# First MLP of a two-layer diffusion block: hidden features completed and squared in their PSUM bank, with all their low parts on VectorE

## The chip, the cores and the metric

The kernel runs on one core of one Trainium2 chip. The metric is the device time of one execution in microseconds (us), as the median over runs. The engines are TensorE (PE; its weight loads are shown apart as PEld), VectorE (DVE), ScalarE (ACT), GpSimd (POOL) and SyncE (SP), which issues most of the DMAs. Each engine works through its own queue in order; semaphores order the engines among each other.

## The reference

Two layers (DEPTH = 2) work on 512 latent tokens x and 256 context tokens ctx of 1024 features, in float32. The change touches the MLP at the end of a layer alone. The context tokens go through the MLP of layer 0 only, since nothing reads them after layer 1.

```python
def squared_relu_mlp(h, w1, w2):
    return jnp.square(jax.nn.relu(h @ w1)) @ w2
...
    for l in range(DEPTH):
...
            h_ctx = h_ctx + cg2 * rmsnorm(squared_relu_mlp(hc2, w_ff1[l], w_ff2[l]), g_post_ff[l])
...
        hx2 = rmsnorm(x, g_pre_ff[l]) * (1.0 + sc2) + sh2
        x = x + g2 * rmsnorm(squared_relu_mlp(hx2, w_ff1[l], w_ff2[l]), g_post_ff[l])
```

## The kernel before

**Two parts.** TensorE takes float32r operands, which hold fewer bits than float32. So each operand is kept as a high part (a copy that is rounded to float32r) and a low part (the value minus the high part), and a product is three products: high by high, high by low, low by high.

**The MLP.** The 4096 hidden features go in 16 groups of 256. In each layer groups 0 and 1 are plain products (`ff1`, L1099 on; tiles h000c, h011x and so on: layer, group, half of the features, kind of token). They are made of 24 matmuls each, for the 256 context tokens (layer 0 only) and for two halves of the latent tokens. Groups 2 to 15 (`wino`, L1171 on) use Winograd's form of Strassen's product for the latent tokens: seven products of twelve matmuls (called 11, 21, t1, t2, t3, t4, 22; tiles w and wt) over sums of weights and sums S of token blocks, from which additions make four quadrants c11, c22, c21 and c12. In layer 0 two plain products for the context tokens (`plain`, tiles wc) come with each group. `hidden` (L1118 on) takes a quadrant or a plain product, and makes Relu (ScalarE), the square as high part (ScalarE, into the tile hx or hc), the square again in place (ScalarE), and the difference as low part. `ff2` then multiplies the hidden features of a group with its rows of w_ff2 (tiles f200x for group 0 and so on) and VectorE adds the result to Y.

**Memory.** PSUM has two banks with the tag S, two with T, three with F and one with V. The plain products of groups 0 and 1 use S alone; the products of `wino` alternate between S and T, so a product takes the bank of the one four before it, where no other step takes a T. The second products use F. Temporaries in SBUF come from the tags h1, h2 and h3 with two buffers each, and the tiles of a tag are handed out in the order of the program text. r of `hidden` is an h1, p1 and u4 are h2, the quadrants c11, c22 and c21 are h3. The sums S of the token blocks (`wino_a`, L943 on, called once before group 2) go through s1 (h1), s2 (h2) and s3 (h3). In layer 0 two of the four etiles and one of the two ptiles hold sums for the rest of the layer. So hx and hc of a group take the buffers of the group before, and are written when its second products have read them.

**Order.** A scheduler sets the order of each engine's queue from the program text, the dependences, the priorities (`tc.high_priority(offset=HP)` around `wino`) and its own estimates of the durations. Second products of one group and first products of the next are therefore mixed. GpSimd and VectorE share the low parts by the table LOADS; its entry for the hidden features of layer 0 is "vpvpvv": two of six on GpSimd. Beside the MLP of layer 0 run the modulations of layer 1: VectorE sums rows of w_ada (L264, L266), as each load arrives.

Of the kernel before, what the change touches and what calls it, by code (L numbers as in the profile page):

```python
# [11 lines left out]
F32 = mybir.dt.float32  # L12
# [6 lines left out]
P = 128  # L19
# [12 lines left out]
# How far the first product of the MLP goes ahead of other work.  # L32
HP = 5
# The engine (v or p) that takes each of the two-operand steps of a hidden group: low parts of the weights of the
# first and second product, differences of weights, low parts of the hidden features.
# [10 lines left out]
# What the tensor engine does beside the attention units of a layer: U, G, F load the weights of a column group  # L46
# of the in-projection and u, g, f project a token block with them, fc, fx step through the Fourier mixing,
# gc, gx load the gates, oc, ox step through the output projection, ada through a modulation.
# [13 lines left out]
def _bc(ap, n, axis):  # L62
    """ap with a broadcast dimension of n put in at free position `axis`."""
    v = ap.unsqueeze(axis)
    shape = list(v.shape)
    shape[axis] = n
    return v.to_broadcast(shape)
# [3 lines left out]
def kernel(ctx: ExitStack, tc: tile.TileContext, a: dict, out: bass.AP):  # L71
# [15 lines left out]
    # Temporaries of a chain come from h1, h2, h3 in this order, so that chains never wait in a circle.  # L87
# [9 lines left out]
    # Streams that run side by side have tiles of their own; within a tag tiles are handed out in program order.  # L97
# [35 lines left out]
    # ------------------------------------------------------------- constants  # L133
# [18 lines left out]
    def rows_in(name, width, pairs):  # L152
        """Rows at given partitions of a zeroed [32, width] tile."""
# [6 lines left out]
    def turned(t, name, use):  # L160
        """Feature-major pieces of four chunks of such rows in PSUM, handed to `use`."""
# [7 lines left out]
    # silu(c), silu(c_ctx) as two columns of a zero-padded stationary operand  # L169
# [37 lines left out]
    # ---------------------------------------------------- common small helpers  # L207
# [4 lines left out]
    def power(o, i, scale, bias, expo):  # L212
        """o = (i * scale + bias) ** expo"""
# [11 lines left out]
    def wunit(src, shape, name, lo_eng=None, part=None, hi_pool=False):  # L225
        """A weight unit in two float32r parts whose sum is the float32 weight."""
# [11 lines left out]
    # ------------------------------------------------------------------ adaLN  # L238
    # modc[l]: feature-major columns for (sh1, sc1, sh2, sc2); gates go to DRAM rows.
# [271 lines left out]
    def layer(l, feats):  # L511
# [659 lines left out]
        def wino(g):  # L1171
# [31 lines left out]
            def tile3(nm_):  # L1203
                return h3([P, n], F32, f"{nm_}{nm}")
# [209 lines left out]
```

## Time and profile before

| | |
|---|---|
| median of 3 runs | 1516.37 us (1515.86 to 1518.47) |
| span of the profiled execution | 1516.8 us |
| TensorE busy | 1429.4 us (94%) |
| VectorE, ScalarE, GpSimd busy | 74%, 49%, 42% |
| MLP of layer 0 in the trace | about 345 to 930 us |
| MLP of layer 1 in the trace | about 1158 us to the end |

The profiled execution has a span of 1516.8 us from its first to its last instruction, 0.4 us more than the median of the runs; no other time of it is given. A busy share is the time in which an engine worked on an instruction. Matmuls overlap in the records: a 128x256 matmul is shown with some 0.28 us, while its successor starts 0.12 us later. In the rows of the trace, "[1.63 <-ACT hi_f L234]" says that the engine was idle for 1.63 us just before the row, until line 234 on ScalarE released it.

### The profile page before, as it was taken

The numbers are of one execution on the slowest core, as the hardware profiler recorded it, in microseconds if no ns is written. First come the engines' busy times: TensorE is split into PE (matmuls) and PEld (weight loads), VectorE is DVE, ScalarE is ACT, GpSimd is POOL, SyncE is SP. The second block draws the span as 40 slices with busy tenths as digits, with TensorE's granted clock in tenths as the row PEclk, the third lists the DMA queues.
The fourth block names the chain that finished last, engine by engine and source line by source line (L and its number), as shares of the span: only waits on it lengthen the run. The fifth ranks groups of instructions, "written<-read, shape, count | busy, mean of one in ns | idle before, by whom it ended". The sixth has DMA issues, their size and how long they took to land. (4 is left out here: it accounts for less than half of the span.)

```text
span 1516.8 us, 24509 instructions
## 1 busy us (share of the span) xinstructions
PE 1429.4 (94%) x9133; PEld 1252.7 (83%) x9133; DVE 1115.8 (74%) x2003; ACT 747.7 (49%) x1673; POOL 644.3 (42%) x608
## 2 busy tenths in 40 slices
PE   7999999999899999999989998999998899999997
PEld 4688798788788878888878887998777788989886
DVE  3366887858687877878777758788757987777685
ACT  3346666556534333343333445476656555554452
POOL 3212636646634333334433546234346644344241
PEclk9999999999999999999999999999998999999999
DMA  9634322435132332325554344213134133223322
GB/s 328 228 122 154 112 74 84 137 115 167 42 100 84 124 111 84 126 70 174 167 172 129 125 160 139 72 55 87 39 100 165 56 112 111 93 89 100 110 84 84
DMA packets 94352, 177.58 MB, mean 117 GB/s; under 512 B 5796, under 2 KB 59524, under 8 KB 94232
## 3 DMA queue, kind: packets, MB, share of 16 engines
q1 hardware_dynamic: 91224, 170.93, 35.0%
q0 software_dynamic: 3008, 5.08, 1.2%
q8 instruction: 72, 1.18, 0.3%
q14 instruction: 48, 0.39, 0.1%
HBM read 166.62 MB, written 9.46 MB: 116 GB/s over the span
## 5 line engine op out<-in xcount | busy, mean ns | idle before, releaser
L1152 POOL TENSOR_TENSOR raw_f<-raw_f,raw_f 128x512 f32<-128x512 f32 x70 | 98.2, 1402 | 107.8 <-DVE raw_f L1152 89.5
L1147 ACT CAST Wf<-raw_f 128x512 fp32r<-128x512 f32 x98 | 60.4, 619 | 118.6 <-DMA raw_f<-in_w_ff 108.4
L266 DVE SCALAR_TENSOR_TENSOR acc<-wa,silu,acc 128x1024 f32<-128x1024 f32 x70 | 96.1, 1391 | 21.7 <-DMA wa<-in_w_ada 21.6
L1148 POOL TENSOR_TENSOR Wf<-raw_f,Wf 128x512 fp32r<-128x512 f32 x28 | 40.1, 1433 | 153.3 <-ACT Wf L1147 153.3
L1195 PE MATMUL wc<-f01c,Wf 128*128 128x256 f32 x672 | 98.5, 286 | 3.4 <-DVE p L1201 3.4
L1195 PEld LDWEIGHTS wc<-f01c,Wf 128*128 128x128 f32 x672 | 91.6, 194 | 7.9 <-DVE p L1201 3.8
L1148 DVE TENSOR_TENSOR Wf<-raw_f,Wf 128x512 fp32r<-128x512 f32 x70 | 62.0, 887 | 41.0 <-ACT Wf L1147 40.9
L234 ACT CAST hi_f<-raw_f 128x1024 fp32r<-128x1024 f32 x72 | 73.8, 1043 | 34.8 <-PE f208c L1247 6.6
L235 POOL TENSOR_TENSOR lo_f<-raw_f,hi_f 128x1024 fp32r<-128x1024 f32 x20 | 54.7, 2735 | 77.7 <-ACT hi_f L234 57.6
L1125 DVE TENSOR_TENSOR hx<-r,hx 128x256 fp32r<-128x256 f32 x98 | 61.5, 630 | 31.2 <-ACT r L1124 31.1
L235 DVE TENSOR_TENSOR lo_f<-raw_f,hi_f 128x1024 fp32r<-128x1024 f32 x52 | 76.6, 1478 | 1.3 <-ACT hi_f L234 1.0
L1123 ACT ACTIVATE hx<-r 128x256 fp32r<-128x256 f32 x112 | 45.4, 413 | 44.4 <-PE f203x L1247 8.7
L1182 PE MATMUL w<-f11x,Wf 128*128 128x256 f32 x336 | 65.1, 283 | 0.0
L1182 PE MATMUL w<-S,Wf 128*128 128x256 f32 x336 | 63.0, 283 | 0.0
L1122 ACT ACTIVATE r<-c 128x256 f32<-128x256 f32 x84 | 34.7, 414 | 55.5 <-DVE c L1201 43.4
L1182 PEld LDWEIGHTS w<-f11x,Wf 128*128 128x128 f32 x336 | 54.7, 191 | 1.5
L1182 PEld LDWEIGHTS w<-S,Wf 128*128 128x128 f32 x336 | 53.0, 191 | 1.7 <-issue 0.4
L1182 PE MATMUL w<-f01x,Wf 128*128 128x256 f32 x336 | 50.4, 284 | 1.9 <-ACT Wf L1147 1.0
L1182 PEld LDWEIGHTS w<-f01x,Wf 128*128 128x128 f32 x336 | 46.4, 191 | 5.3 <-ACT Wf L1147 1.4
L1124 ACT ACTIVATE r<-r 128x256 f32<-128x256 f32 x112 | 45.5, 413 | 1.9
L393 ACT ACTIVATE xvx<-xTx,mod 128x256 f32<-128x256 f32 x64 | 31.6, 560 | 18.2 <-PE xTx L379 11.9
L797 ACT ACTIVATE E0x<-E0x,mx_0x 128x512 f32<-128x512 f32 (+1 forms) x32 | 24.9, 778 | 12.9 <-DVE mx_0x L791 12.7
(1243 smaller groups left out, 4886.1 us busy)
## 6 DMA issues: line engine op xcount, KB each, us to landing
raw_f<-in_w_ff SPq DMA_DIRECT2D x128, 512.0 KB
wa<-in_w_ada SPq DMA_DIRECT2D x80, 512.0 KB
wq<-in_w_ada SPq DMA_DIRECT2D x16, 512.0 KB
raw_out0c<-in_w_out SPq DMA_DIRECT2D x8, 512.0 KB
raw_out0x<-in_w_out SPq DMA_DIRECT2D x8, 512.0 KB
res0x<-xr0x SPq DMA_DIRECT2D x8, 512.0 KB
raw_out1x<-in_w_out SPq DMA_DIRECT2D x8, 512.0 KB
xl0x<-in_x SPq DMA_DIRECT2D x4, 512.0 KB
```

The source lines that it names most:

```text
L234: nc.scalar.copy(hi, raw)
L235: (lo_eng or nc.vector).tensor_tensor(out=lo, in0=raw, in1=hi.bitcast(F32), op=ALU.subtract)
L266: nc.vector.scalar_tensor_tensor(out=acc[r], in0=w, scalar=s, in1=acc[r], op0=ALU.mult, op1=ALU.add)
L1122: nc.scalar.activation(r, src, AF.Relu)
L1123: nc.scalar.activation(hv[:, 0], r, AF.Square)
L1124: nc.scalar.activation(r, r, AF.Square)
L1125: next(lo_h).tensor_tensor(out=hv[:, 1], in0=r, in1=hv[:, 0].bitcast(F32), op=ALU.subtract)
L1147: nc.scalar.copy(t[:, 0], src)
L1148: next(lo).tensor_tensor(out=t[:, 1], in0=src, in1=t[:, 0].bitcast(F32), op=ALU.subtract)
L1152: next(diff).tensor_tensor(out=o, in0=x, in1=y, op=ALU.subtract)
L1182: nc.tensor.matmul(ps, W[w][:, wl, k], A[k // 2][:, k % 2, xh], start=(m == 0), stop=(m == 11))
L1195: nc.tensor.matmul(ps, W[f"{k // 4 + 1}{j + 1}"][:, wl, k % 4], f2["c"].ap(k, xh, 0, CTX), start=(m == 0), stop=(m == 3 * KD - 1))
```

## The change

In layer 0 `hidden` has no tile r any more: Relu and the second square work in place on `src`. That is the PSUM bank of the product for the plain products, and for the quadrants too, since the new function `quadrant` adds the other operand into the bank of the quadrant's last product. The low part reads the bank and is always on VectorE. In layer 1 (`last`) the tiles r stay, the low parts go by the table, and the quadrants lie in h3; the fourth, which was added in place in u4, is now an h3 tile as well. In both layers p1 takes p7 ahead of the quadrant c22 instead of behind it. Comments and doc strings are taken out as well, which moves lines from L1201 on.

```diff
         def hidden(g, kd, j, t0, n, src, nm):
...
             hv = H[g][kd][j][:, :, t0:t0 + n]
-            r = h1([P, n], F32, f"r{nm}")
+            r = h1([P, n], F32, f"r{nm}") if last else src
             nc.scalar.activation(r, src, AF.Relu)
             nc.scalar.activation(hv[:, 0], r, AF.Square)
             nc.scalar.activation(r, r, AF.Square)
-            next(lo_h).tensor_tensor(out=hv[:, 1], in0=r, in1=hv[:, 0].bitcast(F32), op=ALU.subtract)
+            (next(lo_h) if last else nc.vector).tensor_tensor(out=hv[:, 1], in0=r, in1=hv[:, 0].bitcast(F32), op=ALU.subtract)
...
-            def tile3(nm_):
-                return h3([P, n], F32, f"{nm_}{nm}")
+            def quadrant(x, ps, j, t0, name):
+
+                c = h3([P, n], F32, f"{name}{nm}") if last else ps
+                add(c, x, ps)
+                hidden(g, "x", j, t0, n, c, f"{nm}{name}")
 
             p1 = h2([P, n], F32, f"p1{nm}")
             nc.scalar.copy(p1, product("11", a11))
-            p2 = product("21", a12)
-            c11 = tile3("c11")
-            add(c11, p1, p2)
-            hidden(g, "x", 0, 0, n, c11, f"{nm}11")
+            quadrant(p1, product("21", a12), 0, 0, "c11")
             plain(0)
             p5 = product("t1", sums(1))
             add(p1, p1, product("t2", sums(2)))
             u4 = h2([P, n], F32, f"u4{nm}")
             add(u4, p1, p5)
             p7 = product("t3", sums(3))
-            c22 = tile3("c22")
-            add(c22, u4, p7)
-            hidden(g, "x", 1, n, n, c22, f"{nm}22")
             add(p1, p1, p7)
-            p4 = product("t4", a22)
-            c21 = tile3("c21")
-            add(c21, p1, p4)
-            hidden(g, "x", 0, n, n, c21, f"{nm}21")
-            p3 = product("22", sums(4))
-            add(u4, u4, p3)
-            hidden(g, "x", 1, 0, n, u4, f"{nm}12")
+            quadrant(u4, p7, 1, n, "c22")
+            quadrant(p1, product("t4", a22), 0, n, "c21")
+            quadrant(u4, product("22", sums(4)), 1, 0, "c12")
             plain(1)
```

The scheduler makes another order of it. Up to the plain products the queues read the same, and those of the mixing stage of layer 1 do too.

**VectorE, plain products of groups 0 and 1.** L1125 is the low part in `hidden`, L956 and L953 are additions and low parts of the sums S, L396 the low parts of the normalised tokens f01x, L266 the modulation. Before, from the first low part of a latent half (hx<-r000x) on:

```order
L1125 TENSOR_TENSOR hx_4155<-r000x_4329,hx_4155 128x256
L266 SCALAR_TENSOR_TENSOR acc_4726<-wa_4800,silu,acc_4726 128x1024
L266 SCALAR_TENSOR_TENSOR acc_4727<-wa_4800,silu,acc_4727 128x1024
L396 TENSOR_TENSOR f01x_3849<-xvx_4106,f01x_3849 128x2x256
L396 TENSOR_TENSOR f01x_3850<-xvx_4116,f01x_3850 128x2x256
L1125 TENSOR_TENSOR hx_4156<-r001x_4359,hx_4156 128x256
L396 TENSOR_TENSOR f01x_3851<-xvx_4126,f01x_3851 128x2x256
L1125 TENSOR_TENSOR hx_4230<-r010x_4389,hx_4230 128x256
L396 TENSOR_TENSOR f01x_3852<-xvx_4136,f01x_3852 128x2x256
L1125 TENSOR_TENSOR hx_4155<-r000x_4517,hx_4155 128x256
L1148 TENSOR_TENSOR Wf_4827<-raw_f_4820,Wf_4827 128x512
L1152 TENSOR_TENSOR raw_f_4820<-raw_f_4820 128x4x128
```

Now, from the L266 ahead of that low part (hx<-h000x) on:

```order
L266 SCALAR_TENSOR_TENSOR acc_4714<-wa_4788,silu,acc_4714 128x1024
L266 SCALAR_TENSOR_TENSOR acc_4715<-wa_4788,silu,acc_4715 128x1024
L396 TENSOR_TENSOR f01x_3849<-xvx_4106,f01x_3849 128x2x256
L396 TENSOR_TENSOR f01x_3850<-xvx_4116,f01x_3850 128x2x256
L1125 TENSOR_TENSOR hx_4155<-h000x_4300,hx_4155 128x256
L396 TENSOR_TENSOR f01x_3851<-xvx_4126,f01x_3851 128x2x256
L956 TENSOR_TENSOR s_4634<-s_4636,f01x_3851 128x512
L396 TENSOR_TENSOR f01x_3852<-xvx_4136,f01x_3852 128x2x256
L956 TENSOR_TENSOR s_4653<-s_4655,f01x_3852 128x512
L1125 TENSOR_TENSOR hx_4156<-h001x_4329,hx_4156 128x256
L956 TENSOR_TENSOR s_4634<-s_4634,f01x_3851 128x512
L1125 TENSOR_TENSOR hx_4228<-h010x_4358,hx_4228 128x256
```

The low part of h000x stood ahead of two L266 and two L396 and now stands behind them. The first additions L956 now stand among the low parts of the first latent half; before, they came behind the second low part of r010x, that of the second half.

**TensorE, plain products of the context tokens.** h001c and h010c are products of groups 0 and 1, xTx transposes of the normalised latent tokens, f200c second products. Before:

```order
L1106 MATMUL h010c_4232<-f01c_3212,lo_f_4226 128x256
L1106 MATMUL h010c_4232<-f01c_3212,hi_f_4225 128x256 x2
L1106 MATMUL h010c_4232<-f01c_3212,lo_f_4226 128x256
L379 MATMUL xTx_4101<-ident,y0x_3619 128x128
L1247 MATMUL f200c_4425<-hi_f_4294,hc_4154 128x512
L1247 MATMUL f200c_4425<-lo_f_4295,hc_4154 128x512
L1247 MATMUL f200c_4433<-hi_f_4294,hc_4154 128x512
L1247 MATMUL f200c_4433<-lo_f_4295,hc_4154 128x512
L1247 MATMUL f200c_4442<-hi_f_4294,hc_4154 128x512
L1247 MATMUL f200c_4442<-lo_f_4295,hc_4154 128x512
L379 MATMUL xTx_4111<-ident,y0x_3619 128x128
L1106 MATMUL h011c_4262<-f01c_3209,hi_f_4219 128x256 x2
```

Now:

```order
L1106 MATMUL h001c_4186<-f01c_3212,hi_f_4150 128x256 x2
L1106 MATMUL h001c_4186<-f01c_3212,lo_f_4151 128x256
L379 MATMUL xTx_4101<-ident,y0x_3619 128x128
L1240 MATMUL f200c_4417<-hi_f_4290,hc_4154 128x512
L1240 MATMUL f200c_4417<-lo_f_4291,hc_4154 128x512
L1240 MATMUL f200c_4425<-hi_f_4290,hc_4154 128x512
L1240 MATMUL f200c_4425<-lo_f_4291,hc_4154 128x512
L1240 MATMUL f200c_4434<-hi_f_4290,hc_4154 128x512
L1240 MATMUL f200c_4434<-lo_f_4291,hc_4154 128x512
L1106 MATMUL h010c_4230<-f01c_3209,hi_f_4217 128x256 x2
```

The product h010c stood ahead of the first transposition shown and of the six second products; now it stands behind them.

**VectorE, Winograd group 6.** wt are the products t1 to t4, hc the hidden features of the context tokens, lo_f a low part of w_ff2. Before, from the addition of t2 to p on:

```order
L1201 TENSOR_TENSOR p_6254<-p_6254,wt_6332 128x256
L235 TENSOR_TENSOR lo_f_6441<-raw_f_6438,hi_f_6440 128x1024
L1201 TENSOR_TENSOR u_6346<-p_6254,wt_6319 128x256
L1201 TENSOR_TENSOR c_6361<-u_6346,wt_6348 128x256
L1201 TENSOR_TENSOR p_6254<-p_6254,wt_6348 128x256
L1201 TENSOR_TENSOR c_6382<-p_6254,wt_6369 128x256
L1125 TENSOR_TENSOR hx_6225<-r_6363,hx_6225 128x256
L1148 TENSOR_TENSOR Wf_6583<-raw_f_6576,Wf_6583 128x512
```

Now, from the lo_f ahead of that addition on:

```order
L235 TENSOR_TENSOR lo_f_6384<-raw_f_6381,hi_f_6383 128x1024
L1201 TENSOR_TENSOR p_6206<-p_6206,wt_6281 128x256
L1125 TENSOR_TENSOR hc_6175<-wc_6239,hc_6175 128x256
L1201 TENSOR_TENSOR u_6295<-p_6206,wt_6268 128x256
L1201 TENSOR_TENSOR p_6206<-p_6206,wt_6297 128x256
L1201 TENSOR_TENSOR wt_6297<-u_6295,wt_6297 128x256
L1201 TENSOR_TENSOR wt_6316<-p_6206,wt_6316 128x256
L1125 TENSOR_TENSOR hx_6177<-wt_6297,hx_6177 128x256
L1148 TENSOR_TENSOR Wf_6526<-raw_f_6519,Wf_6526 128x512
L1125 TENSOR_TENSOR hx_6176<-wt_6316,hx_6176 128x256
```

The low part of hc is now in this queue, ahead of the additions of t1, t3 and t4; the addition of t3 to p stands ahead of the quadrant c22, and the quadrants are written to wt.

## Rows read from the trace of the kernel before

**Rows 1.** The page's first part: busy time of each engine, its share of the span and its count of instructions.
```profile
PE 1429.4 (94%) x9133; PEld 1252.7 (83%) x9133; DVE 1115.8 (74%) x2003; ACT 747.7 (49%) x1673; POOL 644.3 (42%) x608
```

**Rows 2.** Stretches of the span: start and end, length, busy time (and instructions) of PE, PEld, DVE, ACT and POOL, granted TensorE clock as a share of full speed, DMA share, GB/s.
```profile
357.00:405.00 48.00, 47.57 (x331) 44.47 (x330) 30.74 (x34) 27.59 (x61) 23.60 (x23) 0.98 0.17 56
405.00:890.00 485.00, 457.07 (x2853) 404.13 (x2853) 375.20 (x508) 186.49 (x402) 198.81 (x136) 0.99 0.39 123
1195.00:1487.00 292.00, 287.53 (x1784) 258.73 (x1784) 226.92 (x359) 146.03 (x298) 117.69 (x82) 0.99 0.30 94
424.00:430.00 6.00, 4.05 (x19) 3.55 (x19) 6.00 (x9) 1.04 (x2) 0.00 (x0) 0.75 0.28 87
```

**Rows 3.** Waits of TensorE between 405 and 890 us: who waited for whom, us in total, times, longest.
```profile
PE wc L1195 <- DVE p L1201: 3.4, 2, 2.8
...
PE f205x L1247 <- DVE lo_f L235: 2.3, 1, 2.3
...
PE f206x L1247 <- DVE Y0x L1251: 1.9, 1, 1.9
```

**Rows 4.** TensorE in order of time, 405 to 432 us, the rows with a wait ahead: start, length, operation, count, wait.
```profile
407.81 0.73 PE L1247 MATMUL f201c<-hi_f,hc 128*128 128x512 f32 x2 [1.63 <-ACT hi_f L234]
...
413.60 0.79 PE L1247 MATMUL f201c<-lo_f,hc 128*128 128x512 f32 x1 [3.03 <-DVE lo_f L235]
...
418.69 0.98 PE L1182 MATMUL wt<-S,Wf102t 128*128 128x256 f32 x6 [0.57 <-DVE S L953]
...
420.66 0.98 PE L1182 MATMUL wt<-S,Wf102t 128*128 128x256 f32 x6 [0.99 <-DVE S L953]
...
426.29 2.34 PE L1182 MATMUL wt<-f01x,Wf102t 128*128 128x256 f32 x12 [1.95 <-DVE p L1201]
```

**Rows 5.** VectorE in order of time, 379 to 396 us.
```profile
386.24 0.42 DVE L1125 TENSOR_TENSOR hx<-r000x,hx 128x256 fp32r<-128x256 f32 x1 [6.51 <-ACT r000x L1124]
389.41 0.69 DVE L1148 TENSOR_TENSOR Wf<-raw_f,Wf 128x512 fp32r<-128x512 f32 x1 [2.74 <-ACT Wf L1147]
...
394.38 1.12 DVE L1125 TENSOR_TENSOR hx<-r010x,hx 128x256 fp32r<-128x256 f32 x1 [2.57 <-ACT r010x L1124]
395.54 1.68 DVE L956 TENSOR_TENSOR s<-s,f01x 128x512 f32<-128x512 f32 x1
```

**Rows 6.** VectorE in order of time, 354 to 380 us.
```profile
354.65 2.86 DVE L396 TENSOR_TENSOR f01x<-xvx,f01x 128x512 fp32r<-128x512 f32 x1
...
368.10 0.42 DVE L1125 TENSOR_TENSOR hx<-r000x,hx 128x256 fp32r<-128x256 f32 x1
370.81 2.48 DVE L266 SCALAR_TENSOR_TENSOR acc<-wa,silu,acc 128x1024 f32<-128x1024 f32 x2 [2.30 <-DMA wa<-in_w_ada]
373.21 1.29 DVE L396 TENSOR_TENSOR f01x<-xvx,f01x 128x512 fp32r<-128x512 f32 x2
374.42 1.51 DVE L1125 TENSOR_TENSOR hx<-r001x,hx 128x256 fp32r<-128x256 f32 x1
377.70 1.09 DVE L396 TENSOR_TENSOR f01x<-xvx,f01x 128x512 fp32r<-128x512 f32 x1 [1.77 <-POOL f01x L395]
```

**Rows 7.** TensorE in order of time, 344 to 356 us: the first matmuls of h010c, and the first after it.
```profile
349.41 0.40 PE L1106 MATMUL h010c<-f01c,hi_f 128*128 128x256 f32 x2
...
354.88 0.30 PE L379 MATMUL xTx<-ident,y0x 128*128 128x128 f32 x1 [2.42 <-DVE y0x L370]
```

**Rows 8.** VectorE's groups of instructions between 405 and 890 us: line, operation, tiles, shapes, count, then busy us, mean ns of one, and idle time ahead with what ended it.
```profile
L266 DVE SCALAR_TENSOR_TENSOR acc<-wa,silu,acc 128x1024 f32<-128x1024 f32 x66 | 91.0, 1397 | 19.4 <-DMA wa<-in_w_ada 19.3
...
L1125 DVE TENSOR_TENSOR hx<-r,hx 128x256 fp32r<-128x256 f32 x41 | 31.2, 764 | 16.1 <-ACT r L1124 16.1
```

**Rows 9.** The low parts of line 1125 alone between 357 and 890 us: busy time and count on VectorE and on GpSimd, then clock and DMA.
```profile
357.00:890.00 533.00, 44.13 (x62) 32.49 (x31) 0.99 0.37 117
```

**Rows 10.** Forms of an instruction over the whole span: count, then least, median and greatest duration in ns, first and last start. The first is an addition with an operand in PSUM (L1201), the second the low part from SBUF (L1125), the third a Relu from PSUM (L1122).
```profile
L1201 DVE TENSOR_TENSOR p<-p,wt x56: 403/410/422, 425.8 to 1485.7; 128x256 f32<-128x256 f32 x56
...
L1125 DVE TENSOR_TENSOR hx<-r,hx x98: 409/424/2623, 451.2 to 1490.1; 128x256 fp32r<-128x256 f32 x98
...
L1122 ACT ACTIVATE r011x<-h011x x2: 365/370/374, 377.0 to 396.3; 128x256 f32<-128x256 f32 x2
```

**Rows 11.** ScalarE in order of time, 576 to 584 us, Winograd group 6: the squares of the plain product (hc, r06c), then Relu and second square of c22 (r).
```profile
577.20 0.41 ACT L1123 ACTIVATE hc<-r06c 128x256 fp32r<-128x256 f32 x1
...
578.46 0.41 ACT L1124 ACTIVATE r06c<-r06c 128x256 f32<-128x256 f32 x1
580.21 0.42 ACT L1122 ACTIVATE r<-c 128x256 f32<-128x256 f32 x1 [1.34 <-DVE c L1201]
...
581.11 0.42 ACT L1124 ACTIVATE r<-r 128x256 f32<-128x256 f32 x1
```

**Rows 12.** TensorE in order of time, 577 to 586 us: the last of t2 and the twelve of t3, the twelve of t4, and the first two of the next group's product 11.
```profile
576.97 1.72 PE L1182 MATMUL wt<-S,Wf106t 128*128 128x256 f32 x13
578.52 1.60 PE L1182 MATMUL wt<-f01x,Wf106t 128*128 128x256 f32 x12
...
585.47 0.40 PE L1182 MATMUL w<-f01x,Wf 128*128 128x256 f32 x2
```

**Rows 13.** VectorE in order of time, 577 to 586 us: the low part of w_ff2 and the addition of t3 to p.
```profile
578.10 1.22 DVE L235 TENSOR_TENSOR lo_f<-raw_f,hi_f 128x1024 fp32r<-128x1024 f32 x1
...
580.09 0.41 DVE L1201 TENSOR_TENSOR p<-p,wt 128x256 f32<-128x256 f32 x1
```

## Prediction, made before the changed kernel was run

> **What bounds the kernel now.** I read the busy shares first, then the stretches, then who TensorE waits for inside one stretch. TensorE is busy for 1429.4 of 1516.8 us, VectorE for 74%, GpSimd for 42% [rows 1]. The change issues the same matmuls, so only idle TensorE time, or time at a lower clock, can move the result. The MLP of layer 0 has two stretches. From 357 to 405 us (the first two groups, written as plain products) TensorE is idle for 48.00 - 47.57 = 0.4 us. From 405 to 890 us (the Winograd groups) it is idle for 485 - 457.07 = 27.9 us. The Winograd groups of layer 1 are idle for 292 - 287.53 = 4.5 us, so little is to be won there [rows 2].
>
> The 27.9 us fall into two kinds. Five stalls between 407 and 429 us add to 1.63 + 3.03 + 0.57 + 0.99 + 1.95 = 8.2 us [rows 4]: the second products wait for ScalarE's and VectorE's parts of w_ff2, the first Winograd group for the sums S of the token blocks and for an addition in VectorE's queue. Behind them TensorE is granted less clock: 0.75 over 424 to 430 us [rows 2], between its two levels of 1.2 and 2.4 GHz, and twelve matmuls take 2.34 us there [rows 4] against 1.60 at full clock [rows 12]. With the other short pieces I put that at 1.3 us, so this onset costs 9.5 us. The other 19.7 us are single waits of 0.2 to 2.8 us over 460 us, mostly for VectorE [rows 3].
>
> **The change part by part.** *The sums leave the queue for h1.* In the old kernel the temporaries s1 of the sums share the tag h1 with the r of every hidden(), and tiles of a tag go out in program order. So the first sum on VectorE starts at 395.54, right behind the low part of the last but one r (394.38), although VectorE had been idle for 6.51, 2.74 and 2.57 us shortly before [rows 5]. In the new kernel layer 0 has no r. The new order puts eight additions and two low parts of the sums before the hidden features of the second token half, that is, into that idle time. They leave the stretch from 395 to 425 us, where all five stalls lie and where their place was in front of the low parts for which TensorE waited. I let 8.5 of the 9.5 us go; the bounds are 4.8 (the two waits for parts of w_ff2, 4.7 us, stay) and 9.5.
>
> *Banks held longer in the plain products.* These products alternate between the two banks of S. So far a bank was free after its Relu; now after Relu, two squares and the low part on VectorE. Three products are late by this, read from the new order with times of before. First, h010c needs the low part of h000c, which stands behind the f01x that runs from 354.65 for 2.86 us [rows 6], so it is done at 357.9. The old order ran the 24 matmuls of h010c from 349.41 on, ahead of a wait until 354.88 that had to be waited out anyway [rows 7]; the new order has them behind that wait: 24 x 0.12 us and a rest of 0.5, 3.4 us. Second, h010x needs the low part of h000x, which was done at 368.5 and now stands behind two L266, which wait for a DMA until 370.81, and two L396: done at 374.8 [rows 6]. By then TensorE, 3.4 us late and with nine transposes and second products taken in ahead, has waited about 1.1 us. Third, h011x needs the low part of h001x, which now stands behind an f01x that GpSimd releases at 377.70 [rows 6], two sums and another f01x. With 1.68 us for each sum, as at 395.54 [rows 5], it is done at 383.8, with 0.68 us at 381.2; TensorE is there at about 381.4, so 0 to 2.4 us. The sum is 4.5 to 6.9 us; I take 5.5, and as bounds 3 (only the first) and 7.
>
> *Low parts on VectorE.* Layer 0 has 96 of them, 32 on GpSimd so far. Of the 357 to 890 us they took 44.13 us of VectorE and 32.49 of GpSimd [rows 9]. A low part from SBUF takes 409 ns at best and up to 2623 [rows 10]; over the Winograd stretch the mean is 764 [rows 8]. VectorE's additions with one operand in PSUM lie between 403 and 422 ns, 56 of them, with no slow one [rows 10]. The new low parts have that form, so 96 x 0.42 = 40.3 us: VectorE does all of them in 3.8 us less than its share so far, and GpSimd loses 32 us. Other instructions with two operands in SBUF are slowed less: L266 takes 1.24 us undisturbed [rows 6] and 1.397 in the mean [rows 8], 10 us in all over 66; I estimate 5 us over all such instructions if 15% of GpSimd's work goes. No addition that writes to PSUM is in the trace. I price it as its neighbour that reads PSUM, 0.41 us; at worst I take 0.68, as a sum of double size in rows 5, which would be 56 x 0.27 = 15 us of VectorE and would eat the relief. ScalarE's Relu from a bank takes 0.365 to 0.374 us [rows 10] against 0.42 from SBUF [rows 11], and ScalarE is busy for 49%: nothing. Of the 19.7 us of scattered stalls some 13 hang on VectorE's queue, which gets 2 to 3% shorter; I take 3 us as gain, with bounds 0 and 9.
>
> The Trainium skill speaks against this part: "VectorE: DVE Perf Modes", section "Rules for kernel authors", advises to copy matmul output to SBUF first if many operations follow, and "Perfetto Trace Analysis", section "Optimizing Scalar/DVE Operations", gives VectorE about 60 ns of access overhead on SBUF and 125 on PSUM. By those figures 96 low parts and 56 additions would cost VectorE 152 x 0.065 = 9.9 us more (an estimate), and my 3 us of gain would be nothing. The rows say otherwise: 403 to 422 ns with PSUM against 409 at best without [rows 10].
>
> *Banks held longer in the Winograd groups.* Nine products go round four banks. c22 stays in its bank until its low part. In group 6 of before, p is updated at 580.09 [rows 13], Relu to second square last from 580.21 to 581.53 [rows 11], and with 0.42 us for the low part the bank is free at about 582.4, after the addition to p that now stands ahead; the next user of that bank starts at 585.47 [rows 12]. So this costs nothing while 3 us lie between. The plain product is worse. Its square waits until the second products of the group before have read hc; in group 6 the squares are over at 578.88 [rows 11], and lo_f and an addition stand ahead of the low part [rows 13], so the bank is free at 579.3. Its next user, the product t4, started at 578.52 [rows 12], 0.8 us earlier. The new order has six more matmuls of t2 ahead of t4 there (19 x 0.12 us from 576.97 on, so 579.25), which covers it. I take 0 for it here, and 0.8 us in each of 13 groups, 10.4 us, as upper bound.
>
> *Layer 1* keeps r, engines and banks; p1 is updated before c22, so c22 is late by one addition of 0.41 us [rows 10], and the fourth quadrant takes an h3 tile. Its stretch has 4.5 us of idle time; I take 0.5 us of loss, between -1 and +2.
>
> **Sum.** 1516.8 - 8.5 + 5.5 - 3 + 0.5 = 1511.3 us for this execution. Its span lies 0.4 us above the median of the runs, 1516.37, so the runs should show 1511 us, 0.35% less.
>
> **The rivals.**
> 1. *Slower: the bank of the plain product decides.* If hc is read later than planned, t4 waits in each group: 1511.3 + 10.4 = 1521.7 us, 1521 in the runs. For it speaks that the low part stands in VectorE's queue, which in the old kernel GpSimd took. Against it, the new order leaves room in most groups. It decides from 0.65 us a group (8.5 / 13) on: that is where the time is above 1519.4. The Trainium skill ("Perfetto Trace Analysis", section "Matmuls") asks that independent groups rotate through banks, so that emptying one overlaps the next products; holding banks longer is against that, and no row of before shows a wait for such a chain.
> 2. *No change.* The onset gives back only 4.8, and the late plain products cost their 5.5: 1516.8 - 4.8 + 5.5 - 1 = 1516.5 us. For it: the waits for w_ff2 hang on queues of ScalarE and VectorE that are only in part the sums'.
> 3. *Much faster: the banks of the plain products don't bind*, since ACT and VectorE reach them earlier than I read: 1516.8 - 9.5 + 1 - 6 = 1502.3 us.
>
> **How the numbers follow.** A measurement of this kernel can tell about 0.2%, 3 us, from no change. The forecast (1505 to 1513) gets 0.45, the first rival 0.23, the second 0.2, the third 0.12. So faster by over 0.2% 0.57, within 0.2% 0.2, slower 0.23. The range from 1501 to 1522 leaves out less than 2 in 10: most of the first rival's spread above 1522 and a little of the third. The forecast's own range is 1505 to 1514.
>
> **What would show it right or wrong.** Right: VectorE's sums L956 start near 379 us; no stall over 1 us between 405 and 430 us; TensorE idle for 4 to 7 us between 349 and 393 us, ended by a low part L1125; the low parts at 0.41 to 0.43 us each without slow ones; GpSimd's busy time 32 us down. Wrong: waits of wt or w products for L1125 in group after group (rival 1), or the waits for hi_f and lo_f still there near 410 us (rival 2). The forecast falls if additions into PSUM take far more than 0.42 us, or if the new order makes VectorE wait at the front of its queue for something late that I have not seen.

## Result, and the profile after

The changed kernel takes 1527.83 us (median of 5 runs, 1525.12 to 1531.54) beside 1517.43 us for the kernel before on the same chip: a ratio of 1.0068, 95% interval 1.0051 to 1.0085. It is slower by 0.7%, where 0.35% faster was forecast, and the time lies above the range. The profiled execution has a span of 1523.3 us, 6.5 us more than that of before.

A profile is one execution, and its span lies up to 7.4 us from the median of its kernel's runs. So sizes are taken from the medians below, and places from the traces.

The page's first part and the stretch of the Winograd groups of the changed kernel, in the columns of [rows 1] and [rows 2]:

```profile
PE 1437.3 (94%) x9133; PEld 1259.0 (83%) x9133; DVE 1103.2 (72%) x2035; ACT 734.5 (48%) x1673; POOL 607.9 (40%) x576
```
```profile
405.00:890.00 485.00, 462.72 (x2838) 408.21 (x2837) 352.71 (x525) 175.38 (x401) 163.93 (x106) 0.98 0.39 123
```

VectorE has 12.6 us less work and GpSimd 36.4 us less. TensorE is idle as long as before (1523.3 - 1437.3 = 86.0 us against 87.4), but 7.9 us longer busy with the same matmuls: it works longer at a low clock (granted in the mean 0.977, before 0.985). Its waits from 405 to 890 us, in the columns of [rows 3], the longest:

```profile
PE wt L1182 <- DVE hc L1125: 10.5, 4, 3.6
PE wt L1182 <- DVE p L1201: 3.5, 3, 2.9
PE wc L1195 <- DVE hc L1125: 2.4, 4, 0.8
PE f2010x L1240 <- ACT hx L1123: 2.3, 1, 2.3
```

Fewer and longer waits are left (22.3 us of idle time in this stretch instead of 27.9), and 10.5 + 2.4 = 12.9 us of them are for the low part of the plain product hc. Two of them, and the one in the onset, in TensorE's order of time (columns of [rows 4]):

```profile
424.25 2.37 PE L1182 MATMUL wt<-f01x,Wf102t 128*128 128x256 f32 x12 [2.94 <-DVE p L1201]
757.19 2.93 PE L1182 MATMUL wt<-f01x,Wf1011t 128*128 128x256 f32 x12 [3.04 <-DVE hc L1125]
796.85 2.81 PE L1182 MATMUL wt<-f01x,Wf1012t 128*128 128x256 f32 x12 [3.57 <-DVE hc L1125]
```

Twelve matmuls take 2.4 to 2.9 us behind such a wait, and 1.60 at full clock [rows 12]; over 700 to 800 us the granted clock is 0.92, between the levels of 1.2 and 2.4 GHz:

```profile
700.00:800.00 100.00, 89.47 (x537) 79.59 (x536) 72.78 (x107) 34.60 (x77) 35.36 (x24) 0.92 0.51 159
```

Why hc is late at 757 us is seen on VectorE, in order of time, with GpSimd's and ScalarE's row below:

```profile
750.99 1.28 DVE L266 SCALAR_TENSOR_TENSOR acc<-wa,silu,acc 128x1024 f32<-128x1024 f32 x1 [0.74 <-DMA wa<-in_w_ada]
752.19 0.68 DVE L1244 TENSOR_TENSOR Y0c<-Y0c,f2010c 128x512 f32<-128x512 f32 x1
752.78 2.82 DVE L235 TENSOR_TENSOR lo_f<-raw_f,hi_f 128x1024 fp32r<-128x1024 f32 x1
755.53 1.27 DVE L266 SCALAR_TENSOR_TENSOR acc<-wa,silu,acc 128x1024 f32<-128x1024 f32 x1
756.72 0.41 DVE L1125 TENSOR_TENSOR hc<-wc,hc 128x256 fp32r<-128x256 f32 x1
```
```profile
751.63 2.89 POOL L235 TENSOR_TENSOR lo_f<-raw_f,hi_f 128x1024 fp32r<-128x1024 f32 x1 [8.93 <-ACT hi_f L234]
```
```profile
750.22 0.38 ACT L1124 ACTIVATE wc<-wc 128x256 f32<-128x256 f32 x1
```

The squares were over at 750.60. The low part came 6.1 us later, behind two accumulations of the modulation (L266), an addition to Y and a lo_f that takes 2.82 us while GpSimd makes its own lo_f (1.22 us undisturbed, [rows 13]).

### The profile page after: what moved, and what is told of

The parts are those of the page before. It is cut to its first block, busy times and chain, and to the rows that moved or that the text cites. A ratio compares the mean times of both kernels' runs of the same rounds, so it can differ in the third digit from the quotient of the medians.

```text
span 1523.3 us, 24474 instructions
## 1 busy us (share of the span) xinstructions
PE 1437.3 (94%) x9133; PEld 1259.0 (83%) x9133; DVE 1103.2 (72%) x2035; ACT 734.5 (48%) x1673; POOL 607.9 (40%) x576
## 5 line engine op out<-in xcount | busy, mean ns | idle before, releaser
L266 DVE SCALAR_TENSOR_TENSOR acc<-wa,silu,acc 128x1024 f32<-128x1024 f32 x70 | 92.6, 1340 | 26.8 <-DMA wa<-in_w_ada 26.7
L235 DVE TENSOR_TENSOR lo_f<-raw_f,hi_f 128x1024 fp32r<-128x1024 f32 x52 | 72.6, 1404 | 4.1 <-ACT hi_f L234 4.1
L1122 ACT ACTIVATE w<-w 128x256 f32<-128x256 f32 x28 | 10.2, 365 | 48.5 <-DVE w L1201 48.4
L1122 ACT ACTIVATE wc<-wc 128x256 f32<-128x256 f32 x28 | 10.2, 363 | 44.5 <-PE wc L1195 44.4
L797 ACT ACTIVATE E0x<-E0x,mx_0x 128x512 f32<-128x512 f32 (+1 forms) x32 | 24.9, 777 | 12.9 <-DVE mx_0x L791 12.7
L1201 DVE TENSOR_TENSOR p<-p,wt 128x256 f32<-128x256 f32 x56 | 23.2, 414 | 10.3 <-PE wt L1182 9.6
L797 ACT ACTIVATE E1x<-E1x,mx_1x 128x512 f32<-128x512 f32 (+1 forms) x32 | 24.9, 778 | 11.6 <-DVE mx_1x L791 11.4
```

What stands on the lines that cost most here:

```text
L235: (lo_eng or nc.vector).tensor_tensor(out=lo, in0=raw, in1=hi.bitcast(F32), op=ALU.subtract)
L266: nc.vector.scalar_tensor_tensor(out=acc[r], in0=w, scalar=s, in1=acc[r], op0=ALU.mult, op1=ALU.add)
L797: nc.scalar.activation(e, e, AF.Exp, bias=m, scale=-1.0, accum_out=su[:, h, 0:1])
```

## Experiments

All times are medians. "Base" is the kernel before with all low parts of layer 0's hidden features on VectorE. The interval is that of the ratio to the kernel before, run beside it (1518.3 to 1519.7 us). The intervals reach 1.5 to 3.5 us to either side, and a difference of two rows is known no better than that.

| run | edit | us | ratio, 95% interval |
|---|---|---|---|
| e3_lows_v | base | 1517.1 | 0.9993 (0.9982 to 1.0003) |
| e6_quad_only | base, quadrants in their banks | 1530.1 | 1.0075 (1.0061 to 1.0089) |
| e9_plain_only | base, plain products of the Winograd groups in their bank | 1522.1 | 1.0022 (1.0011 to 1.0032) |
| e8_ff1_only | base, products of groups 0 and 1 in their bank | 1512.8 | 0.9964 (0.9951 to 0.9977) |
| e7_layer1 | before, change of layer 1 alone | 1522.0 | 1.0025 (1.0015 to 1.0035) |
| e1_plain_r | changed, but plain products of the Winograd groups with r in SBUF | 1531.2 | 1.0081 (1.0064 to 1.0097) |
| e2_quad_r | changed, but quadrants with c and r in SBUF | 1522.2 | 1.0024 (1.0014 to 1.0034) |
| e5_ff1_r | changed, but groups 0 and 1 with r in SBUF | 1524.4 | 1.0034 (1.0021 to 1.0047) |
| e10_ff1_rn | base, r of groups 0 and 1 in a tag of its own | 1520.2 | 1.0000 (0.9987 to 1.0014) |
| e11_base_noada | base without modulation | 1488.6 | 0.9792 (0.9770 to 0.9813) |
| e12_quad_noada | e6 without modulation | 1488.0 | 0.9792 (0.9770 to 0.9813) |
| e16_plain_noada | e9 without modulation | 1495.8 | 0.9853 (0.9830 to 0.9875) |
| e13_after_noada | changed, without modulation | 1502.7 | 0.9891 (0.9872 to 0.9909) |
| e17_shift_base | base, modulation shifted | 1517.7 | 0.9992 (0.9978 to 1.0007) |
| e18_shift_quad | e6, modulation shifted | 1532.4 | 1.0087 (1.0070 to 1.0104) |
| e19_shift_after | changed, modulation shifted | 1530.9 | 1.0066 (1.0048 to 1.0083) |
| e14_base_noload | base, modulation without loads | 1514.7 | 0.9978 (0.9966 to 0.9990) |
| e15_quad_noload | e6, modulation without loads | 1526.8 | 1.0055 (1.0039 to 1.0072) |

**One part taken back.** My first theory was rival 1: the plain product's bank holds up t4. Three runs give one part its r in SBUF back, and one moves the low parts alone:

```diff
-            r = h1([P, n], F32, f"r{nm}") if last else src
+            r = h1([P, n], F32, f"r{nm}") if last or own else src
# own=True in the plain products (e1), in the quadrants, with c in h3 (e2), in ff1 (e5)
```
```diff
# e3, on the kernel before
-    (0, 'loh'): "vpvpvv",
+    (0, 'loh'): "v",
```

> The changed kernel, but the plain products of the Winograd groups get r in SBUF back, so that their bank is free after the Relu; quadrants and the products of groups 0 and 1 stay in their banks, all low parts of layer 0 stay on VectorE. Theory (the bank of the plain product, held until its low part, stops t4): the waits of t4 for the low part of hc vanish (10.5 us in four in the changed kernel), with them the lower clock behind them, and the lead of 3 to 4 us that the changed kernel has after group 9 is kept: 1513 to 1516 us. Rival (VectorE's queue as a whole, since it has all low parts): other products wait for VectorE instead, TensorE idles as long in groups 10 to 13, 1523 us or more.

> The changed kernel, but the quadrants lie in h3 again and have r in SBUF; the plain products of all groups stay in their banks, all low parts stay on VectorE. Theory (bank of the plain product): t4 still waits for the low part of hc, 5 to 12 us in all, 1522 to 1530 us. Rival (the quadrants, held in their banks up to their low part, or written there by VectorE, are the cause): the loss goes, 1512 to 1517 us.

> The kernel before with one edit: all low parts of the hidden features of layer 0 on VectorE, still from r in SBUF. Theory (bank of the plain product): no product waits for a low part, so the time is that of the kernel before within 3 us, 1515 to 1521 us. Rival (VectorE's longer queue alone makes the loss): 1523 us or more.

> The changed kernel, but the plain products of groups 0 and 1 get r in h1 back, so their banks are free after the Relu and the sums of the token blocks share a tag with r again. By the terms of the prediction: the 5 us that TensorE idles between 345 and 393 us go, the stalls between 405 and 430 us come back with 7 to 8.5 us, and the rest is as in the changed kernel: 1529 to 1531 us. Rival (the idle time before 393 us is not from the banks): both stay, 1527 us with TensorE idle for 5 us before 393; or (the onset's stalls are not from the tag) 1522 us without stalls over 1 us from 405 to 430 us.

e1 came out at 1531.2 us, no better than the changed kernel: the theory falls as the whole cause. Other products wait in t4's place (wc for an addition to p 8.3 us in three, a modulation product for a quadrant's low part 3.8 us in two). e2 wins back 1527.8 - 1522.2 = 5.6 us, so the quadrants are in it. e3 shows that the longer queue alone costs nothing. e5 was 3.4 us faster where 1 to 3 us slower was expected.

**One part alone.** Since the parts taken back didn't add up, each went alone onto the base:

```diff
# e6: quadrants only (p1 takes p7 ahead of c22, as in the change); e9, e8: at=ps in plain, in ff1
+            def quadrant(x, ps, j, t0, name):
+                c = tile3(name) if last else ps
+                add(c, x, ps)
+                hidden(g, "x", j, t0, n, c, f"{nm}{name[1:]}", None if last else c)
...
-            r = h1([P, n], F32, f"r{nm}")
+            r = h1([P, n], F32, f"r{nm}") if at is None else at
# e7, on the kernel before: for the last layer p1 takes p7 ahead of c22, and c12 is an h3 tile
```

> The kernel before with all low parts of layer 0 on VectorE (1517 us so) and one thing more: the quadrants of layer 0 are completed and squared in their banks, with p1 updated ahead of c22; plain products keep r, layer 1 is as before. Theory (the quadrants' banks, held until the low part, make TensorE follow VectorE's queue): 1522 to 1527 us, with waits of w, wt or wc products for L1125 or additions L1201 in groups 9 to 13. Rival (the quadrants are not the cause, only their sum with the plain products is): 1514 to 1519 us.

> The kernel before with the change of layer 1 alone: p1 takes t3 ahead of c22, c12 is an h3 tile. By the prediction's term (0.5 us): 1518 to 1520 us, beside 1518.5 us for the kernel before. Rival (the 3.7 us that are left when the quadrants get their h3 tiles back are layer 1's): 1521 to 1523 us, with the loss behind 1195 us.

> The kernel before with all low parts of layer 0 on VectorE (1517 us so) and one thing more: the plain products of groups 0 and 1 of layer 0 are squared in their bank, without r. By the terms of the prediction (5.5 us lost before 393 us, 8.5 us won from 405 to 430 us): 1513 to 1516 us. Rival (the run that gave these products their r back was 3.4 us faster, so the trade is a loss): 1519 to 1522 us.

> The kernel before with all low parts of layer 0 on VectorE (1517 us so) and one thing more: the plain products of the Winograd groups are squared in their bank, without r; quadrants and groups 0 and 1 are as before. If this bank stops t4: 1520 to 1527 us, with waits of wt for the low part of hc. Rival (as the run that gave these products their r back was not faster, the bank of the plain product costs nothing by itself): 1514 to 1518 us.

e6 came out 3 us above its range, e7 where its rival had it, e9 as expected: TensorE waits there 9.8 us for the low part of hc (6.7 for wt, 3.1 for wc). The quadrants cost 1530.1 - 1517.1 = 13.0 us, the plain products 5.0, layer 1 3.7; groups 0 and 1 win 4.3, and e8 is faster than both kernels. Together that would be 1517.1 + 13.0 + 5.0 + 3.7 - 4.3 = 1534.5 us; the changed kernel has 1527.8. Where the quadrants and the plain products are both in their banks they cost less than apart: e5 has both and layer 1, which would add up to 1538.8 us, and took 1524.4. Why is open.

TensorE's waits from 405 to 890 us with the quadrants in their banks (e6), the longest:

```profile
PE wc L1195 <- DVE p L1201: 13.9, 5, 5.0
PE wt L1182 <- DVE p L1201: 3.3, 1, 3.3
...
PE w L1182 <- DVE hx L1125: 2.6, 1, 2.6
PE w L1182 <- ACT r08c L1122: 2.6, 1, 2.6
```

The first of these in the base:

```profile
PE wc L1195 <- DVE p L1201: 3.8, 1, 3.8
```

Most of the new waits are ended by additions to p, not by the low part that frees a quadrant's bank (2.6 us for w and 1.5 for a modulation product).

With e7, layer 1 has other waits than before: where the old order had 1.9 and 1.7 us for Y1x at groups 11 and 12, the new one has 2.5 at group 10, 0.9 at group 2 and 1.4 at the end, for the last hx; with three of 0.5 to 0.6 us that is 6.5 us against 3.6. The two longest:

```profile
PE f2110x L1251 <- DVE Y1x L1255: 2.5, 2, 2.1
PE f2114x L1251 <- ACT hx L1123: 1.4, 1, 1.4
```

**The onset without its price.** e10 gives r of groups 0 and 1 a tag that the attention leaves free:

```diff
+ at = tmp.tile([P, n], F32, name=..., tag="rn", bufs=1)
```

> The kernel before with all low parts of layer 0 on VectorE (1517 us so) and one thing more: r of the plain products of groups 0 and 1 is a tile with a tag of its own and one buffer, so that the bank is free after the Relu and the sums of the token blocks still share no tag with r. By the prediction's terms the onset's gain (7 to 8.5 us) comes without the 5 us that the banks cost before 393 us: 1508 to 1511 us, below the 1512.8 us of the run with r in the bank. Rival (one buffer of r holds the bank as long as the low part does): 1512 to 1515 us.

Neither holds, at 1520.2 us. With one buffer, f200c still waits 1.2 us for a low part; the onset has three other waits (1.3, 1.3 and 2.8 us), and group 4 a wait of 3.4 us that e8 has not. What the tag alone gives stays open.

**Without the modulation.** In the slow places accumulations L266 stand ahead of what TensorE waits for. Four runs leave out the modulation beyond the first load of a sixth:

```diff
             for k in range(KD):
+                if k:
+                    for r in rs:
+                        yield
+                    continue
                 w = load(k)
```

> The kernel before with all low parts of layer 0 on VectorE, without the modulation's accumulations: beside the MLP of layer 0 only the first of the eight loads of w_ada of every sixth is left, and its first product (the modulation of layer 1 is wrong, so the output too). It is the reference for the two runs beside it. If the modulation's places in VectorE's queue make most of the scattered waits in layer 0: 1498 to 1508 us.

> The same (no modulation beyond the first load of a sixth, so a wrong output), with the quadrants of layer 0 completed and squared in their banks: the pair to the run before it, as the run with the quadrants alone (1530 us) was to the one with the low parts alone (1517 us). Theory (the quadrants cost 13 us because the additions and low parts that free the banks stand in VectorE's queue behind accumulations that wait for w_ada): within 4 us of its pair. Rival (the banks are held too long whatever stands in that queue): 9 us or more above its pair.

> The changed kernel without the modulation beyond the first load of a sixth (so a wrong output). Theory (VectorE's queue with the accumulations that wait for w_ada): against the run with the low parts alone and no modulation it keeps the 4 us won at groups 0 and 1 and the 3.7 us lost in layer 1, so it is within 4 us of it. Rival (the banks themselves): 9 us or more above it, as the changed kernel is against 1517 us.

> The kernel before with all low parts of layer 0 on VectorE and the plain products of the Winograd groups squared in their bank, without the modulation beyond the first load of a sixth (so a wrong output). Its pair without that bank took 1488.6 us. Theory (this bank costs its time by itself, since lo_f and additions to Y stand ahead of its low part on VectorE too): 1493 to 1500 us, with waits of wc or wt for the low part of hc. Rival (as with the quadrants, only the accumulations make it late): 1486 to 1491 us.

e11 came out 9 us below its range: without the modulation the base is 28.5 us faster. The quadrants cost nothing now (1488.0 against 1488.6 us; 13 us with the modulation). Stretch 405 to 890 us, in the columns of [rows 2]: base and quadrants with the modulation (e3, e6), then without (e11, e12):

```profile
405.00:890.00 485.00, 458.64 (x2856) 405.67 (x2855) 385.23 (x535) 187.77 (x404) 170.32 (x108) 0.98 0.39 123
```
```profile
405.00:890.00 485.00, 446.46 (x2743) 395.40 (x2743) 371.06 (x523) 171.25 (x387) 163.48 (x106) 0.98 0.38 119
```
```profile
405.00:890.00 485.00, 476.19 (x2980) 422.75 (x2980) 333.34 (x497) 198.87 (x430) 179.80 (x125) 1.00 0.26 82
```
```profile
405.00:890.00 485.00, 476.48 (x2977) 422.39 (x2978) 313.98 (x499) 191.68 (x435) 179.46 (x125) 1.00 0.26 82
```

In that stretch TensorE starts 113 matmuls fewer with the quadrants in their banks and idles for 38.5 us instead of 26.4; once the modulation is gone, it starts 3 fewer. The plain product's bank costs its time there too: e16 is 7.2 us above its pair, though its trace shows only one wait of 1.7 us for the low part of hc. e13 is 14.1 us above, as the rival had it; two waits of 3.8 and 3.9 us for the low part of hc stand out. The first, on TensorE, VectorE and GpSimd:

```profile
543.04 2.29 PE L1199 MATMUL wc<-f01c,Wf 128*128 128x256 f32 x13 [3.80 <-DVE hc L1129]
```
```profile
538.95 3.10 DVE L235 TENSOR_TENSOR lo_f<-raw_f,hi_f 128x1024 fp32r<-128x1024 f32 x1
541.98 0.68 DVE L1156 TENSOR_TENSOR raw_f<-raw_f,raw_f 128x512 f32<-128x512 f32 x1
542.58 0.41 DVE L1129 TENSOR_TENSOR hc<-wc,hc 128x256 fp32r<-128x256 f32 x1
```
```profile
538.62 2.35 POOL L235 TENSOR_TENSOR lo_f<-raw_f,hi_f 128x1024 fp32r<-128x1024 f32 x1 [2.33 <-ACT hi_f L234]
```

No accumulation is in it. The squares were over at 537.58 us, and most of the 5.0 us by which the low part is late are lo_f, slowed beside GpSimd's.

**A price of the banks, or of one order?** A neutral edit moves every step of the modulation one second product ahead:

```diff
         ff2_open(1, mtile, mtile)
+        next(ada, None)
         for kd in kinds[::-1]:
```

> A neutral edit on the kernel before with all low parts of layer 0 on VectorE (1517 us): every step of the modulation comes one second product earlier, the work is the same. If the waits hang on how the work is cut, 1514 to 1520 us; if on which instruction happens to stand ahead of which in VectorE's queue, it may be 5 us or more off.

> The same neutral edit (modulation one step earlier) with the quadrants in their banks (1530 us without the shift). If the 13 us of the quadrants are a price of holding banks beside this modulation: 10 to 16 us above the run beside it. If they are the price of one order of the queue: the difference to the run beside it is off by 5 us or more from 13.

> The same neutral edit (modulation one step earlier) on the changed kernel (1527.8 us). If its loss of 9 us against the kernel before is a price of the banks held: 1524 to 1531 us. If it is that of one order of the queue: off by 5 us or more, in either direction.

The base moves by 0.6 us, the quadrants cost 14.7 us and the whole change 13.2 us: the price doesn't hang on one place of the modulation. The longest wait with the shifted quadrants (e18), on VectorE and then TensorE:

```profile
618.37 4.62 DVE L266 SCALAR_TENSOR_TENSOR acc<-wa,silu,acc 128x1024 f32<-128x1024 f32 x2 [0.88 <-DMA wa<-in_w_ada]
622.91 0.68 DVE L1256 TENSOR_TENSOR Y0c<-Y0c,f206c 128x512 f32<-128x512 f32 x1
623.51 1.21 DVE L235 TENSOR_TENSOR lo_f<-raw_f,hi_f 128x1024 fp32r<-128x1024 f32 x1
624.65 2.47 DVE L266 SCALAR_TENSOR_TENSOR acc<-wa,silu,acc 128x1024 f32<-128x1024 f32 x2
627.04 0.41 DVE L1125 TENSOR_TENSOR hc<-r07c,hc 128x256 fp32r<-128x256 f32 x1
627.37 0.41 DVE L1201 TENSOR_TENSOR p<-p,wt 128x256 f32<-128x256 f32 x1
```
```profile
615.86 4.24 PE L1182 MATMUL wt<-S,Wf107t 128*128 128x256 f32 x34
...
627.84 1.44 PE L1195 MATMUL wc<-f01c,Wf 128*128 128x256 f32 x5 [6.30 <-DVE p L1201]
```

Four accumulations take 7.1 us there, and the addition to p for which wc waits stands behind them. In the base with the same shift (e17) four accumulations stand ahead of this addition too, and wc doesn't wait:

```profile
611.83 0.41 DVE L1201 TENSOR_TENSOR p<-p,wt 128x256 f32<-128x256 f32 x1
```
```profile
609.64 0.39 PE L1247 MATMUL f206c<-hi_f,hc 128*128 128x512 f32 x1
...
612.29 3.13 PE L1195 MATMUL wc<-f01c,Wf 128*128 128x256 f32 x24
```

There the second products f206c of the group before lie between t1 and t4, and TensorE comes to wc just as the addition ends. In e18 they are done before, and TensorE runs through t1 to t4 without a break. The addition frees the bank of t2, which neither kernel holds longer than before. So as far as this trace shows, the edit acts in this wait through the order that the scheduler makes of it, not through the time for which a quadrant's bank is held. No run parts the two, and none tests by itself in layer 0 that p1 takes p7 ahead of c22, which comes with the quadrants.

**Waits for w_ada, or the accumulations themselves?** VectorE waits 31.4 us for w_ada in e6, 23.2 in the base. Two runs keep the accumulations and take seven of eight loads away:

```diff
+            w = load(0)
             for k in range(KD):
-                w = load(k)
...
-                        nc.vector.scalar_tensor_tensor(out=acc[r], in0=w, scalar=s, in1=acc[r],
+                        nc.vector.scalar_tensor_tensor(out=acc[r], in0=acc[r], scalar=nhalf[:, 0:1], in1=acc[r],
```

> The kernel before with all low parts of layer 0 on VectorE, with every accumulation of the modulation still on VectorE at its length, but on its own sum in place of a row of w_ada: only the first of the eight loads of a sixth is left (so a wrong output). Reference for the run beside it; 1488.6 us without accumulations and 1517 us with loads are the ends: if most of the 28 us between are waits for w_ada, 1490 to 1503 us, if they are VectorE's work, 1503 to 1517 us.

> The same (accumulations without loads, so a wrong output) with the quadrants in their banks. If the 13 us of the quadrants come from the waits for w_ada at the front of VectorE's queue: within 5 us of the run beside it. If the accumulations' own length (1.3 us each) is enough: 9 us or more above it.

The waits for w_ada are nearly gone (2.7 us) and the quadrants still cost 1526.8 - 1514.7 = 12.1 us: the price doesn't need the loads. An accumulation takes 1613 ns in the mean in e14 and 1362 in the base, so this pair has more of VectorE's work. And in e15 the bank itself shows: three waits of w, 15.4 us in all, are ended by the low part of a quadrant. The longest, on TensorE, VectorE and TensorE:

```profile
619.80 1.60 PE L1182 MATMUL wt<-S,Wf107t 128*128 128x256 f32 x12
```
```profile
634.37 0.42 DVE L1201 TENSOR_TENSOR wt<-u,wt 128x256 f32<-128x256 f32 x1
...
638.57 0.41 DVE L1125 TENSOR_TENSOR hx<-wt,hx 128x256 fp32r<-128x256 f32 x1
```
```profile
639.04 2.93 PE L1182 MATMUL w<-f01x,Wf 128*128 128x256 f32 x12 [8.60 <-DVE hx L1125]
```

The product t3 was done at 621.4 us. VectorE completed c22 in its bank 13 us later and made its low part at 638.57, and a product of the next group waited for that.

## Why the prediction was wrong, and where it was right

**The onset and groups 0 and 1: right in the net, in part by luck.** A net gain of 8.5 - 5.5 = 3.0 us was forecast; e8, which has only this part, shows 4.3. The sums L956 start at 379.4 us, as read from the order. But both terms came out smaller. Of the three late products only the first shows: the wait before 357 us is 5.30 us in the changed kernel instead of 2.42 [rows 7], and y0x ends it, not a low part L1125. For the low parts of h000x and h001x TensorE waits 0.2 us at most. Of the five stalls of [rows 4] one over 1 us is left, 2.94 at 424.25, where none was forecast, and from 405 to 430 us TensorE idles for 3.4 us instead of 8.2:

```profile
405.00:430.00 25.00, 21.57 (x132) 19.26 (x131) 22.59 (x23) 10.16 (x20) 13.59 (x9) 0.93 0.34 109
```

**The low parts: right in price, too high in worth.** With PSUM as operand they take 419 to 424 ns in the median and 429 at most; from SBUF on VectorE (e3) the mean is 730 ns. So VectorE is relieved by more than the sum said, and the 3 us for it did not come: e3 gives 1 us, within what can be told from nothing, and what the operands in PSUM add to that no run shows by itself. The bound of 0.68 us for an addition into PSUM stands in no row of [rows 5], where a sum of double size takes 1.68 us; nothing hangs on it. The Trainium skill ("SBUF — State Buffer", section "Who interferes with whom") says that a VectorE instruction with two inputs in SBUF contends with a GpSimd instruction that reads SBUF, and that one with at most one such input, outside the two-port modes, does not. The runs agree: lo_f takes 2.8 to 3.1 us beside GpSimd's against 1.2, and the low parts from PSUM show no slow one.

**Banks held longer in the Winograd groups: the step that failed.** "So this costs nothing while 3 us lie between", for the quadrants, is 13.0 us in e6. "I take 0 for it here", for the plain product, is 5.0 us in e9 and 7.2 without the modulation, inside the bound of 10.4. The rule of the Trainium skill that stood beside rival 1 ("Perfetto Trace Analysis", section "Matmuls") agrees with that. Of the two ways that the other rule of the Trainium skill names ("VectorE: DVE Perf Modes", section "Rules for kernel authors"), copying out first would have been the better choice here, though no overhead of PSUM shows in a duration. Both zeros were read from group 6 (577 to 586 us), the quadrants' from c22 alone, and the 579.3 us for the plain product's bank leave out the low part's own 0.41 us. In group 6 they hold: in the changed kernel t4 starts there at 576.50 us without a wait. But that was the place where the price could not be seen. VectorE's accumulations L266 before the change, by stretches of about a group (start and end, length, busy time and count, then clock and DMA):

```profile
550.00:586.00 36.00, 2.48 (x2) 1.00 0.30 103
586.00:620.00 34.00, 12.05 (x8) 1.00 0.36 109
620.00:655.00 35.00, 7.43 (x6) 1.00 0.37 119
655.00:690.00 35.00, 2.04 (x2) 1.00 0.28 86
690.00:725.00 35.00, 11.81 (x9) 1.00 0.59 186
725.00:760.00 35.00, 8.77 (x6) 1.00 0.48 157
760.00:795.00 35.00, 8.93 (x7) 0.96 0.51 159
```

The stretch of group 6 has two, as has one other; the rest have six to nine. [Rows 8] told of 66 of 1.4 us with 19.4 us of idle time ahead, and I used them only to price VectorE's relief, not to ask what a bank would wait for behind them. Rival 1 had the place: t4 waits for the low part of hc, 10.5 us in four waits. It named one of two holders, the one that costs less alone, and its chance of 0.23 was too low for a cost that I had read from one group of 14. Nor did the sum ask what order the scheduler would make in the other groups: the longest waits of e6 and e18 are for additions to p, which free a bank that no quadrant holds.

**Layer 1: mis-sized.** 0.5 us was forecast, bounds -1 and +2; e7 shows 3.7. I priced the 0.41 us by which c22 is late and not the waits of the second products for Y1x in the other order.

**The clock** belongs to the loss: the changed kernel idles no longer in all, but behind its three waits of 2.9 to 3.6 us shown above twelve matmuls take 2.4 to 2.9 us, which the sum priced at nothing.

**Open:** how much of the quadrants' 13 us is the time that their banks are held (shown in e15) and how much the order that the scheduler makes of the edit (shown in e18). Open too is why two parts in their banks together cost less than apart with the modulation, and more without: e13, which also has layer 1 and groups 0 and 1, is 14.1 us above its pair, the single parts 7.2 and -0.6.

## What to carry to other kernels

A PSUM bank that is freed by the last step of a chain on a shared queue can cost what stands ahead of that step in any group, not only the chain's own 2 us: look at every group, above all at those where another stream (here the modulation) has its share of the queue. Copying out early, here r and c in SBUF, costs VectorE time that shows in no wait, and was the faster way in the Winograd groups. Where a scheduler makes the order, an edit also moves what covers a wait, as the second products did in e17 and not in e18. A gain in busy time of an engine that is waited for is worth nothing if the same edit puts it on the way to freeing a bank. What paid was the part before the Winograd groups (e8): 0.36% faster than the kernel before.

## Not expected of the hardware

With the same idle time TensorE's busy time rose by 7.9 us. Waits of 2.9 to 3.6 us had a lower clock behind them (twelve matmuls in up to 2.93 us against 1.60). But the length of a wait alone doesn't tell it. In the changed kernel the granted clock is 0.72 over 714 to 720 us and 0.57 over 834 to 838 us, behind waits of 1.2 and 1.8 us, and 1.00 over 510 to 514 us, behind one of 2.1 us. Before the change waits of 2.3 and 1.9 us [rows 3] lie in stretches with 1.00 (550 to 620 us above). And an addition that writes into PSUM, which no row of before showed, takes about as long as one that reads it: 422 to 428 ns in the median for the four quadrants, 414 for p.
